# The weight-quarter sums of the FFN's seven products, from DVE to POOL

## The chip, the core and the metric

The kernel runs as one program on one core of a Trainium2 chip. The metric is the time of one execution on the device, in microseconds; the median of three runs is taken. The engines named below are those of the profile: PE multiplies matrices, PEld is its weight load, DVE is the vector engine, ACT the scalar engine, POOL the GpSimd engine, and SP issues the DMAs.

## What is computed

Two layers, each with a token mixer (retention, chunked attention and differential attention, gated and merged) and a feed-forward network (FFN). The change lies in the second product of the FFN, 512 tokens by 2816 hidden channels by 1024 model channels, in float32:

```python
for l in range(DEPTH):                         # 2 layers
    ...
    x = _layer_norm(DEEPNORM_ALPHA * x + mix, ln1_g[l], ln1_b[l])
    u = jnp.einsum('bsd,df->bsf', x, w_ffn_in[l])          # 512 x 1024 by 1024 x 5632
    u_gate, u_up = jnp.split(u, 2, axis=-1)
    ffn = jnp.einsum('bsf,fd->bsd', jax.nn.silu(u_gate) * u_up, w_ffn_out[l])
    x = _layer_norm(DEEPNORM_ALPHA * x + ffn, ln2_g[l], ln2_b[l])
```

## The kernel before

**Numbers as pairs.** A float32 operand is carried as a rounded part (`hi`, made on ACT) and what is left of it (`lo`, made on DVE). A product of two such operands is three matmuls, `mm3` in L106 to L108: hi by hi, and the two mixed products. A 512-column matmul is the unit of PE's work.

**Items.** The whole program is a list of items: the weight blocks that an item needs, and a function that does its matmuls. `run_items` keeps three blocks staged (`AHEAD`): at the start of an item it fetches the block of the item two further on. To fetch is to load float32 weights by DMA into one of three buffers `st`, cast them to `wh` on ACT and subtract to `wl` on DVE, each in two halves of 128x1024 elements. There are three buffers each of `wh` and `wl` too, so a cast waits until PE has done the item that last used its buffer. The compiler schedules the instructions of an engine; their order is not quite that of the source.

**The FFN.** The 2816 hidden channels are 22 blocks of 128. An item `u_ffn(i)` makes one of them from 48 matmuls, and `ffn_done` (L965 to L967) applies the gate. The last six blocks go through an ordinary product. The first sixteen form two groups of eight (`GROUPS`), and each group's share of the second product is made with seven products in place of eight (Winograd's form of Strassen's method): token halves and hidden halves on one side, quarters of the weight on the other.

**The hidden side.** When the second block of a pair is there, `Quarters` makes the sums of token halves (L217 to L220), and splits each into hi and lo. The part `q` is the plain quarter that product `m1` takes; its lo half is made by a DVE instruction at L98.

**The weight side.** `Halves` makes, for each group, the seven operands from four loaded quarters W(i, j) of 512x512 (i the half of the hidden rows, j the half of the output columns), each 128 partitions by 2048 elements. `b11` loads W(0,0) into a buffer of its own, `sa`, of which there is one. `t1` adds W(0,1) to it in place, and `t2` adds W(1,1) to that, in place again. `b21` and `b22` are plain quarters. `t3` is W(0,1) + W(1,1), made in the buffer of W(0,1), and `t4` is made from W(1,0) and the sum still in `sa`. Each sum is two instructions of 128x1024 elements on DVE (L163 and L195). `block` then casts and subtracts (`Staged`, L207 and L208).

**The order around the change.** Seven items `([operand], product)` from `fout_items`, in the order b11 with m1, t1 with y, t2 with x, b21, b22, t3, t4, each of 24 matmuls, alternate with `u_ffn` items of the next group (after the second group, with those of the last six blocks). In each layer both groups begin with m1, right behind the `u_ffn` item whose result is its last operand. The product with `t4` is "h"; `plus` adds products to the residual stream `z` or subtracts them.

Of the kernel before, what the change touches and what calls it, by code (L numbers as in the profile page):

```python
# [15 lines left out]
ALU = mybir.AluOpType  # L16
# [37 lines left out]
def trunk(ctx, tc, x_in, w_in, ret_norm_g, da_norm_g, lq1, lk1, lq2, lk2, w_a, w_b, w_c, b_merge, w_out,  # L54
          ln1_g, ln1_b, w_ffn_in, w_ffn_out, ln2_g, ln2_b, rel, rope_ret, rope_da, decay, out):
    nc = tc.nc
# [15 lines left out]
    def g(dt=F32, name="g"):  # L72
        return gp.tile([P, 512], dt, tag="g", name=name)
# [4 lines left out]
    def bank(name="ps"):  # L78
        return psp.tile([P, 512], F32, tag="ps", name=name)
# [25 lines left out]
    def mm3(ps, lh, ll, rh, rl, start, stop):  # L105
        nc.tensor.matmul(ps, lh, rh, start=start, stop=False)  # L106
        nc.tensor.matmul(ps, lh, rl, start=False, stop=False)  # L107
        nc.tensor.matmul(ps, ll, rh, start=False, stop=stop)  # L108
# [31 lines left out]
    class Halves:  # L140
# [19 lines left out]

        def add(self, t, u):
            for s in self.parts():
                nc.vector.tensor_add(t[:, s], t[:, s], u[:, s])  # L163

        def block(self, t):
            return Staged(t, self.kh, self.parts())
# [23 lines left out]
            return self.block(c)  # L190

        def t4(self):
            b, a = self.load(1, 0), self.__dict__.pop("a")
            for s in self.parts():
                nc.vector.scalar_tensor_tensor(b[:, s], a[:, s], -1.0, b[:, s], op0=ALU.mult, op1=ALU.subtract)  # L195
            return self.block(b)

    class Staged:
# [278 lines left out]
    def layer(l):  # L477
# [7 lines left out]
        v = {}  # L485
# [424 lines left out]
        def load_res(src):  # L910
            x1["z"] = [[g(name="z") for _ in range(2)] for _ in range(NT)]
            for t in range(NT):
                load_rows(x1["z"][t], src[P * t:P * t + P])
# [85 lines left out]
        def plus(t, hf, ps, op, final=False):  # L999

            z = x1["z"][t][hf]
            if (t, hf) in x2["fresh"]:
                x2["fresh"].remove((t, hf))
                nc.vector.scalar_tensor_tensor(z, z, ALPHA, ps, op0=ALU.mult, op1=op)
            else:
                nc.vector.tensor_tensor(z, z, ps, op=op)  # L1006
            if final:
                x2["n"].stats(t, hf)

        def fout_items(gi):  # L1010

            r0, kh = GROUPS[gi]
            hv = Halves(w_ffn_out[l], r0, kh)
            w = {}

            def run(name, j, wt):
                ps = bank("pf")
                for k in range(kh):
                    hi, lo = hid[r0 + k].use[name]
                    sl = slice(P * j, P * j + P)  # L1020
                    mm3(ps, hi[:, sl], lo[:, sl], wt.hi[:, k], wt.lo[:, k], k == 0, k == kh - 1)
                return ps

            def m1(wt):
                if gi == 0:
                    load_res(saved[2 * l])
                    x2["fresh"] = {(t, hf) for t in range(NT) for hf in range(2)}
                for j in range(2):
                    ps = run("m1", j, wt)
                    w[j] = g(name="w")  # L1030
                    nc.scalar.copy(w[j], ps)
                    plus(j, 0, ps, ALU.add)

            def y(wt):
                for j in range(2):
                    ps = run("y", j, wt)
                    w["y", j] = g(name="wy")
                    nc.scalar.copy(w["y", j], ps)

            def x(wt):  # L1040
                for j in range(2):
                    ps = run("x", j, wt)
                    u = w.pop(j)
                    nc.vector.tensor_sub(u, ps, u)
                    plus(2 + j, 0, u, ALU.subtract)
                    nc.vector.tensor_add(u, u, w.pop(("y", j)))
                    plus(2 + j, 1, u, ALU.add)
                    plus(j, 1, u, ALU.add)

            def one(name, i, hf, op):  # L1050
                def fn(wt):
                    for j in range(2):
                        plus(2 * i + j, hf, run(name, j, wt), op)
                return fn

            def gg(wt):
                for j in range(2):
                    ps = run("g", j, wt)
                    plus(2 + j, 1, ps, ALU.add)
                    plus(2 + j, 0, ps, ALU.subtract)  # L1060

            return [([hv.b11], m1), ([hv.t1], y), ([hv.t2], x), ([hv.b21], one("m2", 0, 0, ALU.add)),
                    ([hv.b22], one("v", 0, 1, ALU.add)), ([hv.t3], gg), ([hv.t4], one("h", 1, 0, ALU.subtract))]

        def fout_rest(hf):

# [41 lines left out]
        for gi, (r0, kh) in enumerate(GROUPS):  # L1108
            later = ids[:2 * GROUPS[gi + 1][1] if gi + 1 < len(GROUPS) else FT - REST]
            del ids[:len(later)]  # L1110
            for it in fout_items(gi):
                item(*it)
                if later:
                    item(*u_ffn(later.pop(0)))
            for i in later:
                item(*u_ffn(i))
# [60 lines left out]
```

## Time and profile before

| | us |
|---|---|
| median of three runs | 1956.7 (1955.91 to 1957.65) |
| the profiled execution, whole | 1958.14 |
| its span, first to last instruction | 1956.4 |
| PE busy in the span | 1932.8 |
| DVE busy | 1195.5 |
| ACT busy | 836.1 |
| POOL busy | 50.1 |
| mean granted PE clock | 0.997 |

The span is what the profile sees of the execution; the time of the execution holds 1.7 us more around it. PE's matmuls overlap one another, so a busy PE need not be one without small waits; those are read from the starts of its matmuls and from the waits of its weight loads.

### The profile page before, as it was taken

How to read it: one execution, taken by the hardware profiler on the slowest of the kernel's cores; microseconds unless marked ns; L12 is line 12 of the kernel's file. 1: busy time of each engine (PE TensorE's matmuls, PEld its weight loads, DVE VectorE, ACT ScalarE, POOL GpSimd, SP SyncE). 2: the span in 40 equal slices, each digit the busy share in tenths (PEclk: the TensorE clock that was granted, in tenths of full speed). 3: DMA queues.
4: the chain of work that ended last, by engine and by line, in shares of the span. 5: the costliest groups of instructions: out<-in, count | busy, mean ns of one | idle time of the engine just before them, and what ended most of it. 6: DMA issues, size and time to landing. Idle time of an engine off the chain costs nothing. (4 is left out here: it accounts for less than half of the span.)

```text
span 1956.4 us, 24330 instructions
## 1 busy us (share of the span) xinstructions
PE 1932.8 (99%) x9506; PEld 1634.9 (84%) x9506; DVE 1195.5 (61%) x2158; ACT 836.1 (43%) x1503; POOL 50.1 (3%) x73
## 2 busy tenths in 40 slices
PE   7999999999999999999999999999999999999998
PEld 7888888888888888888898888888888888888886
DVE  4654555577656666756585544655775575675656
ACT  3443445476533433333163344545664343432330
POOL 0000000000001000000000000000000000000000
PEclk9999999999999999999999999999999999999999
DMA  6322323222145444434442223222321543444341
GB/s 220 110 81 82 119 81 98 81 77 96 55 129 168 123 126 132 130 107 140 151 144 99 82 87 102 76 92 75 94 89 46 194 129 108 129 139 142 96 134 51
DMA packets 228535, 215.80 MB, mean 110 GB/s; under 512 B 7118, under 2 KB 179268, under 8 KB 228420
## 3 DMA queue, kind: packets, MB, share of 16 engines
q1 hardware_dynamic: 228420, 214.26, 34.9%
q8 instruction: 74, 1.21, 0.3%
q14 instruction: 41, 0.34, 0.1%
HBM read 205.84 MB, written 8.39 MB: 110 GB/s over the span
## 5 line engine op out<-in xcount | busy, mean ns | idle before, releaser
L106 PE MATMUL pt<-xTh,wh 128*128 128x512 f32 (+1 forms) x1632 | 604.2, 371 | 2.9 <-ACT xTh L90 2.9
L108 PE MATMUL pt<-xTh,wl 128*128 128x512 f32 (+1 forms) x1632 | 601.8, 369 | 0.0
L107 PE MATMUL pt<-xTl,wh 128*128 128x512 f32 (+1 forms) x1632 | 601.6, 369 | 0.2 <-DVE xTl L96 0.2
L136 DVE TENSOR_TENSOR wl<-st,wh 128x1024 fp32r<-128x1024 f32 (+1 forms) x314 | 354.3, 1145 | 177.8 <-ACT wh L135 177.6
L135 ACT CAST wh<-st 128x1024 fp32r<-128x1024 f32 (+1 forms) x314 | 301.8, 990 | 318.0 <-PE pt L107 156.7
L106 PEld LDWEIGHTS pt<-xTh,wh 128*128 128x128 f32 x1632 | 308.1, 189 | 53.1 <-ACT xTh L90 3.1
L108 PEld LDWEIGHTS pt<-xTh,wl 128*128 128x128 f32 x1632 | 308.4, 189 | 52.1 <-DVE wl L136 0.2
L107 PEld LDWEIGHTS pt<-xTl,wh 128*128 128x128 f32 x1632 | 308.7, 189 | 50.3 <-DVE xTl L96 0.5
L106 PE MATMUL pn<-wh,xTh 128*128 128x512 f32 x384 | 150.9, 393 | 0.0
L108 PE MATMUL pn<-wh,xTl 128*128 128x512 f32 x384 | 149.6, 390 | 0.0
L107 PE MATMUL pn<-wl,xTh 128*128 128x512 f32 x384 | 149.6, 390 | 0.0
L967 DVE TENSOR_TENSOR fth<-fth,pt 128x512 f32<-128x512 f32 x44 | 30.2, 687 | 128.6 <-PE pt L108 128.6
L108 PEld LDWEIGHTS pn<-wh,xTl 128*128 128x128 f32 x384 | 72.1, 188 | 15.2
L106 PEld LDWEIGHTS pn<-wh,xTh 128*128 128x128 f32 x384 | 72.1, 188 | 14.1
L107 PEld LDWEIGHTS pn<-wl,xTh 128*128 128x128 f32 x384 | 72.2, 188 | 14.1
L965 ACT ACTIVATE fth<-pt 128x512 f32<-128x512 f32 x44 | 26.3, 598 | 122.8 <-PE pt L108 122.8
L269 ACT COPY sw<-pt 32x512 f32<-32x512 f32 (+1 forms) x96 | 55.6, 580 | 31.0 <-PE pt L108 29.7
L966 DVE SCALAR_TENSOR_TENSOR fth<-fth,pt 128x512 f32<-128x512 f32 x44 | 30.2, 686 | 62.6 <-ACT fth L965 62.6
L207 ACT CAST wh<-st 128x1024 fp32r<-128x1024 f32 x32 | 32.1, 1050 | 74.4 <-PE pt L107 74.4
L321 ACT ACTIVATE cE<-cE,mx 128x512 f32<-128x512 f32 (+1 forms) x64 | 35.3, 553 | 65.1 <-DVE mx L320 65.1
L106 PE MATMUL pt<-oah,wh 128*128 128x512 f32 x128 | 50.8, 397 | 0.0
L108 PE MATMUL pt<-oah,wl 128*128 128x512 f32 x128 | 50.0, 390 | 0.0
(234 smaller groups left out, 3019.4 us busy)
## 6 DMA issues: line engine op xcount, KB each, us to landing
st<-in_w_in SPq DMA_DIRECT2D x55, 1024.0 KB
st<-in_w_ffn_in SPq DMA_DIRECT2D x88, 512.0 KB
st<-in_w_ffn_out SPq DMA_DIRECT2D x28, 1024.0 KB
st<-in_w_in SPq DMA_DIRECT2D x32, 512.0 KB
st<-in_w_branch_a SPq DMA_DIRECT2D x8, 1024.0 KB
st<-in_w_out SPq DMA_DIRECT2D x8, 1024.0 KB
saved<-z SPq DMA_DIRECT2D x24, 256.0 KB
z<-saved SPq DMA_DIRECT2D x24, 256.0 KB
```

The lines of the kernel that those rows point to most:

```text
L106: nc.tensor.matmul(ps, lh, rh, start=start, stop=False)
L107: nc.tensor.matmul(ps, lh, rl, start=False, stop=False)
L108: nc.tensor.matmul(ps, ll, rh, start=False, stop=stop)
L135: nc.scalar.copy(self.hi[:, a:b], st[:, a:b])
L136: nc.vector.tensor_sub(self.lo[:, a:b], st[:, a:b], f(self.hi[:, a:b]))
L207: nc.scalar.copy(self.hi[:, s], st[:, s])
L269: nc.scalar.copy(sw[half * b:half * b + half], ps[half * o:half * o + half])
L321: nc.scalar.activation(e, e, AF.Exp, bias=nm, accum_out=sums[:, nt:nt + 1])
L965: nc.scalar.activation(t, pg, AF.Tanh, scale=0.5)
L966: nc.vector.scalar_tensor_tensor(t, t, 1.0, pg, op0=ALU.add, op1=ALU.mult)
L967: nc.vector.tensor_mul(t, t, pu)
```

## The change

The four sums of each group move to POOL, and `t4` becomes the plain sum W(1,0) plus the sum in `sa`, where it was that sum negated. Product h is then added where it was subtracted. So 24 instructions at L163 change their engine, and 8 at L195 change engine and operation; the number of instructions and their sizes stay.

```diff
         def add(self, t, u):
             for s in self.parts():
-                nc.vector.tensor_add(t[:, s], t[:, s], u[:, s])
+                nc.gpsimd.tensor_add(t[:, s], t[:, s], u[:, s])
...
         def t4(self):
-            b, a = self.load(1, 0), self.__dict__.pop("a")
-            for s in self.parts():
-                nc.vector.scalar_tensor_tensor(b[:, s], a[:, s], -1.0, b[:, s], op0=ALU.mult, op1=ALU.subtract)
+            b = self.load(1, 0)
+            self.add(b, self.__dict__.pop("a"))
             return self.block(b)
...
             return [([hv.b11], m1), ([hv.t1], y), ([hv.t2], x), ([hv.b21], one("m2", 0, 0, ALU.add)),
-                    ([hv.b22], one("v", 0, 1, ALU.add)), ([hv.t3], gg), ([hv.t4], one("h", 1, 0, ALU.subtract))]
+                    ([hv.b22], one("v", 0, 1, ALU.add)), ([hv.t3], gg), ([hv.t4], one("h", 1, 0, ALU.add))]
```

## The prediction, written before the result was known

> **What bounds the kernel now.** I read the page's busy times first, then the busy time by stage, then the tile `q` with what waited for it, then PE's and DVE's timelines where that wait is.
>
> ```profile
> PE 1932.8 (99%) x9506; PEld 1634.9 (84%) x9506; DVE 1195.5 (61%) x2158; ACT 836.1 (43%) x1503; POOL 50.1 (3%) x73
> ...
> 740.00:890.00 150.00, 150.00 (x662) 123.99 (x662) 97.74 (x129) 53.24 (x69) 0.00 (x0) 1.00 0.41 120
> 1700.00:1890.00 190.00, 190.00 (x840) 157.09 (x839) 121.40 (x154) 66.34 (x84) 0.00 (x0) 1.00 0.42 127
> ```
>
> PE is the bound. In the two stretches where the sums lie (span, then PE, weight load, DVE, ACT, POOL busy), PE is busy all of the time: 662 matmuls in 150 us, one every 0.227 us. DVE is at 65% and POOL does nothing. So the 32 sums that leave DVE free no time by themselves. PE can only lose, or win back waits too small to make it idle, and the profile shows one kind of these:
>
> ```profile
> its engine sat idle before it (us, times) until:
>   DVE q L98: 1.2, 4
> who waited for it (us, times):
>   PEld pf L108: 1.2, 4
> ...
> 724.00 0.39 PE L107 MATMUL pf<-wl,q 128*128 128x512 f32 x1
> 724.26 0.73 PE L108 MATMUL pf<-wh,q 128*128 128x512 f32 x2
> 724.83 0.40 PE L106 MATMUL pt<-xTh,wh 128*128 128x512 f32 x1
> ...
> 1816.42 0.73 PE L108 MATMUL pf<-wh,q 128*128 128x512 f32 x2
> ```
>
> Four times, once per group and layer, the last two matmuls of product m1 wait 0.3 us each time for the lo half of `q` from DVE. At 724.26 they follow their forerunner by 0.26 us instead of 0.227. This is a place without slack: every microsecond that DVE is later with `q` is a microsecond of PE. What DVE does just ahead of it:
>
> ```profile
> 721.18 1.22 DVE L208 TENSOR_TENSOR wl<-sa,wh 128x1024 fp32r<-128x1024 f32 x1
> 722.32 0.42 DVE L219 TENSOR_TENSOR sb<-fth,sa 128x256 f32<-128x256 f32 x1
> 722.65 1.22 DVE L208 TENSOR_TENSOR wl<-sa,wh 128x1024 fp32r<-128x1024 f32 x1
> 723.79 0.42 DVE L98 SCALAR_TENSOR_TENSOR q<-fth,q 128x256 fp32r<-128x256 f32 x1
> 724.73 1.22 DVE L163 TENSOR_TENSOR sa<-sa,st 128x1024 f32<-128x1024 f32 x1
> ...
> 1815.95 0.42 DVE L98 SCALAR_TENSOR_TENSOR q<-fth,q 128x256 fp32r<-128x256 f32 x1
> ```
>
> DVE ends `q` at 723.79 + 0.42 = 724.21, and the matmul starts 0.05 us later. The two L208 make `wl` from t1 in `sa`, and the sum for t2 overwrites `sa`, half by half. On DVE that sum came behind `q`, at 724.73. It needs only the first L208, which ends at 721.18 + 1.22 = 722.40.
>
> **The change part by part.** What it removes:
>
> ```profile
> L163 DVE TENSOR_TENSOR sa<-sa,st x16: 1215/1219/1228, 703.0 to 1822.7; 128x1024 f32<-128x1024 f32 x16
> L163 DVE TENSOR_TENSOR st<-st x8: 1218/1220/1227, 772.4 to 1865.9; 128x1024 f32<-128x1024 f32 x8
> L195 DVE SCALAR_TENSOR_TENSOR st<-sa,st x8: 1218/1222/1227, 783.2 to 1877.0; 128x1024 f32<-128x1024 f32 x8
> ```
>
> DVE loses 16 x 1.219 + 8 x 1.220 + 8 x 1.222 = 39.0 us. None of it lies ahead of a wait of PE (the sum at 724.73 is behind `q`), so it is worth nothing; 1.2 us, the four waits together, is the most that could be won. The sign of t4 and of h changes no instruction's size: nothing.
>
> What it adds is 32 sums on POOL. No such sum is in this trace. The nearest rows:
>
> ```profile
> 0.73 0.20 POOL masks.py:197 MEMSET ident<- 128x128 f32 x1 [0.29 <-POOLq L1166]
> 0.87 0.10 POOL L69 MEMSET mhalf<- 128x4 f32 x1
> 1.15 0.29 POOL masks.py:199 TENSOR_SCALAR_AFFINE_SELECT ident<-ident 128x128 f32<-128x128 f32 x1
> ```
>
> Writing costs (0.20 - 0.10) / 124 = 0.8 ns a column; reading one operand and writing costs (0.29 - 0.10) / 124 = 1.5 ns, so a read adds about 0.7 ns. Two reads and a write are 2.2 to 2.3 ns, or 2.3 to 2.4 us for 1024 columns with 0.1 us of start. From below, the write alone would be 0.8 us; from above, twice the one-operand price is 3.2 us. I take 2.3 us, from the row with a read in it. The Trainium skill, "GPSIMD Engine Reference", section 3.1, measures a 2048-column fp32 add at 4.497 us against 2.293 on the vector engine; half of that, an estimate from the page, is 2.25 us, and no row here shows it.
>
> *Is the staging still in time?* Now an item's cast on ACT waits for POOL, and the cast's neighbours on ACT queue behind it. The rows of the tightest sums:
>
> ```profile
> 735.77 2.00 ACT L207 CAST wh<-sa 128x1024 fp32r<-128x1024 f32 x2 [4.60 <-PE pt L107]
> ...
> 772.37 2.36 DVE L163 TENSOR_TENSOR st<-st 128x1024 f32<-128x1024 f32 x2
> ...
> 783.15 2.36 DVE L195 SCALAR_TENSOR_TENSOR st<-sa,st 128x1024 f32<-128x1024 f32 x2 [2.37 <-DMA st<-in_w_ffn_out]
> ...
> 784.73 2.00 ACT L207 CAST wh<-st 128x1024 fp32r<-128x1024 f32 x2 [4.66 <-PE pt L107]
> ...
> 801.05 2.01 ACT L207 CAST wh<-st 128x1024 fp32r<-128x1024 f32 x2 [4.66 <-PE pt L107]
> ```
>
> t2 may start at 722.4 and is cast at 735.77: 13.3 us for 4.6. t3 has from 772.37 at the latest to 784.73, 12.3 us. t4 waits for its data until 783.15 and has 17.9 us. Behind each cast stand another 10 us and more: PE takes the block two items after its buffer came free, 48 + 24 matmuls or 16.3 us later, and the cast (2.0) and the subtraction (two of 1.22) take about 4.5. So the sums themselves are hidden by PE, even at twice the price. The loads that wait for a buffer which a sum reads move by 2 or 3 us inside the same slack. On POOL's own queue nothing waits behind a sum but other sums:
>
> ```profile
> 970.60 0.54 POOL L379 TENSOR_TENSOR rs<-rs,mhalf 128x1 f32<-128x1 f32 x1 [334.93 <-DVE rs L378]
> ```
>
> *What does a sum on POOL do to the DVE instructions beside it?* Here is the price of the change. The trace has small POOL instructions that read, beside DVE:
>
> ```profile
> 610.67 0.55 POOL L379 TENSOR_TENSOR rs<-rs,mhalf 128x1 f32<-128x1 f32 x1 [69.45 <-DVE rs L378]
> ...
> 624.74 0.69 DVE L422 TENSOR_TENSOR z<-z,bc 128x512 f32<-128x512 f32 x1
> 625.33 2.36 DVE L136 TENSOR_TENSOR wl<-st,wh 128x1024 fp32r<-128x1024 f32 x2
> 627.61 0.43 DVE L96 TENSOR_TENSOR xTl<-lnt,xTh 128x256 fp32r<-128x256 f32 x1
> 624.90 3.53 POOL L379 TENSOR_TENSOR rs<-rs,mhalf 128x1 f32<-128x1 f32 x1 [6.42 <-DVE rs L378]
> ...
> 982.15 0.68 DVE L422 TENSOR_TENSOR z<-z,bc 128x512 f32<-128x512 f32 x1
> 982.75 2.36 DVE L136 TENSOR_TENSOR wl<-st,wh 128x1024 fp32r<-128x1024 f32 x2
> 982.37 0.85 POOL L379 TENSOR_TENSOR rs<-rs,mhalf 128x1 f32<-128x1 f32 x1 [5.32 <-DVE rs L378]
> ```
>
> Alone, the one-column power takes 0.55 us (610.67). Beside a DVE instruction that reads two SBUF tensors it ends 0.39 us after that instruction: 982.37 + 0.85 = 983.22, against L422's end at 982.83. At 624.90 it got through only when the whole run of such instructions was over: it ends at 628.43, the last of them at 628.04. So POOL's read and DVE's two-tensor read exclude each other for the length of an instruction; POOL may get in between two of them (982.83) or be passed over at three boundaries (625.43 to 627.7). What a long POOL read does to DVE, this trace cannot show: POOL read one column here. From below it costs DVE nothing; from above, DVE stands until the sum is done, up to 3.2 us. I take the second kind at the likely price, since what excludes in one direction by whole instructions should do so in the other.
>
> Now the four places. The first half of t2's sum is released at 722.40 and asks for its operands while L219 (two SBUF tensors) runs, until 722.74. If POOL gets in there, the second L208 begins at 722.74 + 2.3 = 725.04 instead of 722.65, 2.4 us late, and `q` with it. If POOL is passed over there and gets in at the next boundary, between L208 and `q`, `q` is late by as much. The second half of the sum waits for the second L208 and comes too late to get ahead of `q`. So m1's last two matmuls start 2.3 us late (between 2.4 and a little less, as a part of POOL's 2.3 us is start-up): 4 x 2.3 = **9.2 us**. Nothing gives this back, as PE has no idle time behind it. Elsewhere a DVE delay of 2.3 us lies inside the 10 us above.
>
> The Trainium skill, "SBUF — State Buffer", section "Who interferes with whom", says that a vector instruction with two SBUF inputs contends with a GpSimd instruction that reads SBUF, and that whichever starts first holds the shared port for its whole instruction. The first direction agrees with the power that ended 0.39 us after DVE; the case at 624.90, passed over three times, doesn't fit a strict order of issue. By the rule the sum here is the 9.2 us above; without it, nothing.
>
> **The sum.** 0 for the work removed, 0 for the staging, + 9.2 for four delays of `q`. The profiled execution (1958.14, span 1956.4 and 1.7 around it) would become 1967.3; it lies 1.4 above the median of the runs, so the runs should have a median of 1956.7 + 9.2 = **1965.9 us**.
>
> **The rivals.**
>
> *DVE keeps the port until `q` is through, or POOL gives way within its sum.* Then the change is invisible: 1956.7, 1955.5 at best. For it: at 624.90 DVE kept POOL out over three boundaries, and only two lie ahead of `q`. Against: at 982.83 POOL got in at the first, between the same kinds of instruction.
>
> *The two share the port.* If DVE goes at half speed beside POOL, the second L208 and `q` (1.64 us together) lengthen by 0.8 to 1.6 us less the overlap; some 0.8 us at four places is 3 us, 1960. No row speaks for it: a one-column read would not have to wait for an instruction's end.
>
> *It gets faster.* For 4 us or more PE would have to be waiting somewhere for DVE, and only 1.2 us of such waits is there. A changed order of instructions would have to bring it.
>
> *Staging late.* If POOL's sums are starved by DVE's dense runs, a cast comes late. It decides from the point where two halves of t2 take over 13 us (cast) plus 10 (PE): 11 us for one half where I count 2.3. Each further microsecond would be one of PE, in up to 16 items; at 1 us each, 1972.7. DVE at 65%, with pauses such as the 2.37 us before 783.15, makes it unlikely.
>
> *The change doesn't do what it says.* All 32 sums go through the edited lines, so DVE must fall by 39 us; I see no way around that.
>
> **How the numbers follow.** Delay of `q` by whole sums: 0.55. DVE first or POOL yielding: 0.30. Shared: 0.09. Staging late: 0.03. Faster: 0.03. A measurement of this kernel tells about 0.2%, or 3.9 us, from no change. Slower by more: 0.55 + 0.03 + 0.02 of the shared case = 0.60. Within: 0.30 + 0.07 = 0.37. Faster: 0.03. The delay case alone reaches from four delays of 1.5 us (POOL holding DVE up only for its two reads, 2 x 0.7 ns x 1024) to four of 3.1 (the dear sum without its start), 1962.7 to 1969.1. To take in the second case, without which over 2 in 10 would be left out, the range goes from 1955.8 to 1969.5.
>
> **What would show it.** Right: POOL has 32 more instructions; one of them begins at each of the four places about 0.1 us after the first L208; the second L208 or `q` ends some 2.3 us late; and PEld's wait for `q` is 9 to 10 us over four times, not 1.2. DVE instructions beside POOL look longer than 1.22 us, or begin late. Wrong: PEld's wait for `q` stays at 1.2 us; or POOL's halves last much longer than 2.4 us at these places and begin or end only behind `q`. If the compiler places `q` ahead of the second L208, the argument falls too.

## The result and the profile after

| | before | after |
|---|---|---|
| median of four runs, us | 1956.45 (1955.91 to 1957.65) | 1970.46 (1967.56 to 1971.22) |
| span of the profiled execution, us | 1956.4 | 1969.4 |

The ratio is 1.0068, with a 95% interval from 1.0051 to 1.0085: the changed kernel is 14.0 us slower. Line numbers behind L195 are one lower in it; L208 is now L207. In the experiments the numbers shift with each edit, so the same subtraction is L207 to L210 there.

The page's busy times, and the POOL sums in the groups by line (busy time, mean duration in ns, idle time before them):

```profile
PE 1939.0 (98%) x9506; PEld 1638.7 (83%) x9506; DVE 1210.5 (61%) x2126; ACT 835.9 (42%) x1503; POOL 133.1 (7%) x105
...
L163 POOL TENSOR_TENSOR sa<-sa,st 128x1024 f32<-128x1024 f32 x16 | 41.1, 2574 | 270.3 <-DVE wl L207 270.3
L163 POOL TENSOR_TENSOR st<-st,sa 128x1024 f32<-128x1024 f32 x8 | 22.2, 2795 | 42.3 <-DMA st<-in_w_ffn_out 42.3
L163 POOL TENSOR_TENSOR st<-st 128x1024 f32<-128x1024 f32 x8 | 22.1, 2781 | 180.2 <-DMA st<-in_w_ffn_out 180.2
```

All 32 sums are on POOL, at 2.6 to 2.8 us each. DVE has 32 instructions fewer, and yet it is busy 15 us longer (1210.5 for 1195.5): those that are left have become longer. What waited for `q`, in the view of that tile:

```profile
its engine sat idle before it (us, times) until:
  DVE q L98: 18.2, 8
who waited for it (us, times):
  ACT wh L135: 15.7, 4
  PEld pf L108: 9.9, 4
  PE pf L108: 8.3, 4
```

The weight load now waits 9.9 us for `q`, four times, where it waited 1.2. PE's own 8.3 us are the same four waits, seen at the matmul. The timelines of DVE and POOL at the first place (start, duration, instruction):

```profile
719.98 1.22 DVE L207 TENSOR_TENSOR wl<-sa,wh 128x1024 fp32r<-128x1024 f32 x1
721.11 0.42 DVE L218 TENSOR_TENSOR sb<-fth,sa 128x256 f32<-128x256 f32 x1
721.45 3.41 DVE L207 TENSOR_TENSOR wl<-sa,wh 128x1024 fp32r<-128x1024 f32 x1
724.78 0.41 DVE L98 SCALAR_TENSOR_TENSOR q<-fth,q 128x256 fp32r<-128x256 f32 x1
725.12 2.87 DVE L98 SCALAR_TENSOR_TENSOR q2l<-fth,q2h 128x512 fp32r<-128x512 f32 x1
```
```profile
721.27 2.50 POOL L163 TENSOR_TENSOR sa<-sa,st 128x1024 f32<-128x1024 f32 x1 [15.57 <-DVE wl L207]
724.94 2.50 POOL L163 TENSOR_TENSOR sa<-sa,st 128x1024 f32<-128x1024 f32 x1 [1.16 <-DVE wl L207]
```

The first half of t2's sum begins 0.07 us after the end of the first L207 (719.98 + 1.22 = 721.20), while L218 runs. Then the second L207 takes 3.41 us in place of 1.22: it is held for 2.19 us, and `q` comes that much later. POOL's sum ends at 721.27 + 2.50 = 723.77, and the subtraction 1.09 us after that: DVE stood until POOL was through. The second half of the sum begins while `q` runs and holds the next instruction, q2l, for which PE does not wait. Then PE:

```profile
722.80 0.39 PE L107 MATMUL pf<-wl,q 128*128 128x512 f32 x1
725.25 0.73 PE L108 MATMUL pf<-wh,q 128*128 128x512 f32 x2 [2.06 <-DVE q L98]
...
726.20 0.63 PE L107 MATMUL pt<-xTl,wh 128*128 128x512 f32 x1
726.63 0.63 PE L108 MATMUL pt<-xTh,wl 128*128 128x512 f32 x1
727.05 0.63 PE L106 MATMUL pt<-xTh,wh 128*128 128x512 f32 x1
...
729.70 0.39 PE L107 MATMUL pt<-xTl,wh 128*128 128x512 f32 x1
```

Up to the wait, and again from 729.5 on, a matmul begins every 0.227 us. Between 726.20 and 727.05 it is 0.43 us. Less than a microsecond behind its wait PE fell to half speed, and it kept that for some microseconds. The busy times by stretch have the granted clock with it; the columns are span, PE, weight load, DVE, ACT and POOL, each with its instructions, then the granted clock:

```profile
722.46:725.87 3.41, 1.35 (x7) 0.80 (x6) 3.41 (x3) 0.00 (x0) 2.25 (x2) 1.00 0.00 0
725.87:729.28 3.41, 3.41 (x10) 2.67 (x9) 3.41 (x4) 2.96 (x4) 1.57 (x1) 0.50 0.06 10
729.28:732.70 3.42, 3.42 (x17) 2.82 (x16) 2.18 (x2) 0.00 (x0) 0.00 (x0) 1.00 1.05 391
```

For the 3.41 us from 725.87 on, the granted clock is 0.50. In them 10 matmuls run instead of 17 (each count takes in those that overlap an edge), so 7 x 0.227 = 1.6 us are lost. The clock is halved for one such stretch behind each of the four waits of this execution.

**Where the time went.** The waits are 9.9 - 1.2 = 8.7 us. The four halved stretches are 4 x 1.6 = 6.4 us. Together that is 15.1 us, for a span that is 13.0 us longer. Of the difference, 1.5 us is in the other waits of the weight load (18.2 us in sum before, 16.7 after), which lie outside the FFN's sums. The last 0.6 us by which the parts are too large stays unassigned; the profile before has a halved stretch of its own near its start (shown further down), where the changed one has the full clock, and what that is worth was not measured.

### The profile page after: what moved, and what is told of

It is laid out like the page before. It is cut to its first block, busy times and chain, and to the rows that moved or that the text cites. A ratio compares the mean times of both kernels' runs of the same rounds, so it can differ in the third digit from the quotient of the medians.

```text
span 1969.4 us, 24355 instructions
## 1 busy us (share of the span) xinstructions
PE 1939.0 (98%) x9506; PEld 1638.7 (83%) x9506; DVE 1210.5 (61%) x2126; ACT 835.9 (42%) x1503; POOL 133.1 (7%) x105
## 5 line engine op out<-in xcount | busy, mean ns | idle before, releaser
L966 DVE TENSOR_TENSOR fth<-fth,pt 128x512 f32<-128x512 f32 x44 | 30.2, 687 | 143.5 <-PE pt L108 143.3
L163 POOL TENSOR_TENSOR sa<-sa,st 128x1024 f32<-128x1024 f32 x16 | 41.1, 2574 | 270.3 <-DVE wl L207 270.3
L207 DVE TENSOR_TENSOR wl<-st,wh 128x1024 fp32r<-128x1024 f32 x32 | 51.0, 1625 | 2.6 <-ACT wh L206 2.6
```

What stands on the lines that cost most here:

```text
L163: nc.gpsimd.tensor_add(t[:, s], t[:, s], u[:, s])
L207: nc.vector.tensor_sub(self.lo[:, s], st[:, s], f(self.hi[:, s]))
L966: nc.vector.tensor_mul(t, t, pu)
```

## The experiments

The theory after the traces: the whole loss is the first half of t2's sum getting ahead of `q`, in the four places, and PE pays for the wait twice, by its length and by a halved clock behind it. The first rival is that every sum on POOL costs its share; the second, that t2 gives the four waits alone and the other sums the rest.

**Only t2 back on DVE** (t1, t3 and t4 stay on POOL):

```diff
         def t2(self):
-            self.add(self.a, self.load(1, 1))
+            u = self.load(1, 1)
+            for s in self.parts():
+                nc.vector.tensor_add(self.a[:, s], self.a[:, s], u[:, s])
```

> Changed kernel with the sum for t2 back on DVE; t1, t3 and t4 stay on POOL (24 of the 32 sums). Theory (the whole loss is the first half of t2's sum holding DVE up ahead of q, and what PE loses by that wait): 1956.5, within 2 us of before, and the weight load waits for q about 1.2 us over four times. Rival 1 (every sum on POOL costs its share, by holding DVE up or by late staging): three quarters of the 14 us stay, about 1967. Rival 2 (only the four waits come from t2, some 9 us, and the rest from the other sums): about 1961.

Measured: 1957.05 us, ratio to before 0.9998 (0.9989 to 1.0008). The tile `q`:

```profile
  PEld pf L108: 1.2, 4
```

The wait is that of before, and 24 sums on POOL cost nothing that can be measured. Both rivals fall. The sums do hold DVE up here too (the longest subtraction from `sa` still takes 3.42 us), but PE waits for nothing that comes late by it. So it is the place of the hold that costs.

**Only t2 on POOL**, the same edit the other way round in the kernel before: `nc.gpsimd.tensor_add` for t2, the other sums on DVE.

> Kernel before with only the sum for t2 on POOL (8 of the 32 sums). Theory: the whole loss, 1968 to 1971, with four waits of 2.5 us for q and the clock halved for 3.4 us behind each. Rival 1 (every sum its share): a quarter of it, 1960. Rival 2: 1965.5, without the part that the other sums bring.

Measured: 1968.08 us, ratio 1.0055 (1.004 to 1.007). The wait for `q` and the DVE timeline at the first place:

```profile
  PEld pf L108: 9.9, 4
```
```profile
721.87 3.41 DVE L210 TENSOR_TENSOR wl<-sa,wh 128x1024 fp32r<-128x1024 f32 x1
```

Eight of the 32 sums bring the whole of the waits, to a tenth of a microsecond, and 11.3 of the 14.0 us. One thing was not as expected: in this profile the clock is halved behind one of the four waits only, and the span is 1965.7. That led to the last run below, the changed kernel once more.

**t2 as one sum of 2048 columns**, all sums on POOL. It must wait for both subtractions from `sa`:

```diff
         def t2(self):
-            self.add(self.a, self.load(1, 1))
+            u = self.load(1, 1)
+            nc.gpsimd.tensor_add(self.a, self.a, u)
```

> Changed kernel, all sums on POOL, but t2's as one instruction of 2048 columns, which must wait for both subtractions from sa and so starts when q is already running on DVE. Theory: no wait of PE, 1956.5 within 2 us, though POOL adds as much as in the changed kernel. Rivals 1 and 2 (work on POOL costs by its amount): 1965 to 1971. If POOL got ahead of q after all, the wait would be about 5 us and the time near 1980.

Measured: 1956.84 us, ratio 0.9998 (0.9988 to 1.0008). DVE and POOL at the first place:

```profile
723.04 1.22 DVE L208 TENSOR_TENSOR wl<-sa,wh 128x1024 fp32r<-128x1024 f32 x1
724.17 0.42 DVE L98 SCALAR_TENSOR_TENSOR q<-fth,q 128x256 fp32r<-128x256 f32 x1
```
```profile
724.34 6.53 POOL L178 TENSOR_TENSOR sa<-sa,st 128x2048 f32<-128x2048 f32 x1 [17.04 <-DVE wl L208]
```

The sum now starts while `q` runs, `q` keeps its 0.42 us, and the loss is gone. POOL does the same work. What costs is when it starts, not how much it is. This is the change as it could have been made, and it is as fast as the kernel before, not faster: DVE's freed time had no taker.

**A shorter first part.** Two kernels cut t2's sum so that less of it can get ahead of `q`: 512 columns and then 1536, or 768 and then the rest in two pieces. The 512 cut:

```diff
         def t2(self):
-            self.add(self.a, self.load(1, 1))
+            u = self.load(1, 1)
+            for s in (slice(0, 1), slice(1, self.kh)):
+                nc.gpsimd.tensor_add(self.a[:, s], self.a[:, s], u[:, s])
```

> Changed kernel with t2's sum cut into 512 and 1536 columns: the part that can get ahead of q is half as long. Theory for the wait: q is 1.25 to 1.3 us late at four places, 5 us. Clock part, first reading (the clock is halved for 3.4 us behind a wait only if the wait fills most of such a stretch): not at 1.3 us, so 1961.5. Second reading (any wait of a microsecond brings it): 1.7 us more at each place, 1968. If the loss does not go with the length of the first part: 1970.

> Changed kernel with 768 columns of t2's sum first (the rest waits for both subtractions). Between 512 columns (waits of 1.4 us, no halved clock) and 1024 (2.5 us, halved behind some or all): the waits should be 1.9 to 2.0 us, 6.5 us more than before in sum. Clock theory with a chance that grows with the wait: none to two of the four places with the clock halved, at 1.6 us each: 1963 to 1966.5. If the clock is only a matter of 2 us and more: 1963.3.

Measured: 1961.32 us (ratio 1.0023, 1.0013 to 1.0032) and 1963.84 us (1.0031, 1.0017 to 1.0044). The second subtraction on DVE, the first part on POOL and the wait, with 512 columns first:

```profile
720.87 2.31 DVE L209 TENSOR_TENSOR wl<-sa,wh 128x1024 fp32r<-128x1024 f32 x1
```
```profile
720.69 1.41 POOL L179 TENSOR_TENSOR sa<-sa,st 128x512 f32<-128x512 f32 x1 [15.57 <-DVE wl L209]
```
```profile
  PEld pf L108: 5.5, 4
```

and with 768:

```profile
721.14 2.88 DVE L209 TENSOR_TENSOR wl<-sa,wh 128x1024 fp32r<-128x1024 f32 x1
```
```profile
720.96 1.97 POOL L179 TENSOR_TENSOR sa<-sa,st 128x768 f32<-128x768 f32 x1 [15.57 <-DVE wl L209]
```
```profile
  PEld pf L108: 7.8, 4
```

The waits go with the length of the first part. In neither profile is the clock halved behind a wait, and the times are near those expected for that: 1961.5 with 512 columns, by the first reading, and 1963.3 with 768.

**Which part of POOL's work holds DVE?** In two kernels made from the kernel before, the sum for t2 is left out: `sa` is set to zero by POOL, or overwritten with the loaded quarter, in the same two halves released at the same moment. The edits are shown against the kernel with t2 alone on POOL; with the memset the quarter is not loaded either.

```diff
-                nc.gpsimd.tensor_add(self.a[:, s], self.a[:, s], u[:, s])
+                nc.gpsimd.memset(self.a[:, s], 0.0)
...
-                nc.gpsimd.tensor_add(self.a[:, s], self.a[:, s], u[:, s])
+                nc.gpsimd.tensor_copy(self.a[:, s], u[:, s])
```

> Kernel before, with t2's sum left out and both halves of sa set to zero by POOL, released by the same subtraction at the same moment. If POOL's reads are what holds DVE up: DVE's subtraction keeps its 1.22 us, no wait beyond the old 1.2 us in total, 1956.8. If any POOL instruction with 1024 columns holds it up: about 0.8 to 1 us late at four places, 1960 to 1961.

> Kernel before, with t2's sum replaced by a copy of the loaded quarter into sa on POOL: one operand read where the sum reads two. Reads theory, each read taking its time on the port: the copy lasts 1.0 to 1.7 us, DVE's subtraction is as much longer, and with four waits of that length the time is 1961 to 1963.5. If a copy's single read goes past DVE's: 1956.8. If the hold has a fixed length: 1966 or more.

Measured: 1957.1 us with the memset (ratio 1.0, 0.9991 to 1.001), 1960.52 with the copy (1.0017, 1.0008 to 1.0027). DVE and POOL with the memset:

```profile
721.54 1.21 DVE L209 TENSOR_TENSOR wl<-sa,wh 128x1024 fp32r<-128x1024 f32 x1
```
```profile
721.34 0.96 POOL L178 MEMSET sa<- 128x1024 f32 x1 [86.78 <-DVE wl L209]
```

With the copy, DVE's subtraction, POOL's copies as a group, and the wait:

```profile
721.42 2.06 DVE L210 TENSOR_TENSOR wl<-sa,wh 128x1024 fp32r<-128x1024 f32 x1
```
```profile
L179 POOL COPY sa<-st 128x1024 f32<-128x1024 f32 x8 | 9.3, 1161 | 423.6 <-DVE wl L210 423.6
```
```profile
  PEld pf L108: 4.5, 4
```

A write of 0.96 us beside DVE costs DVE nothing; one read stream holds it for 2.06 - 1.22 = 0.84 us, two streams for 2.19. In all four kernels whose POOL instruction reads, the hold is that instruction's length less 0.31 or 0.32 us: 0.84 of 1.16 for the copy, 1.09 of 1.41, 1.66 of 1.97 and 2.19 of 2.50 for the sums. The copy's length lay in the 1.0 to 1.7 us expected. DVE's subtraction was to be longer by all of it and was longer by 0.84 us, so the time lay half a microsecond under the expectation.

**Not every DVE instruction is held.** The changed kernel's own trace shows the other side, where t4's sum runs beside a gate product, which reads one operand from PSUM (`pt`):

```profile
1889.77 0.69 DVE L966 TENSOR_TENSOR fth<-fth,pt 128x512 f32<-128x512 f32 x1 [4.12 <-PE pt L108]
1890.67 2.54 DVE L207 TENSOR_TENSOR wl<-st,wh 128x1024 fp32r<-128x1024 f32 x1 [0.21 <-ACT wh L206]
1893.13 3.41 DVE L207 TENSOR_TENSOR wl<-st,wh 128x1024 fp32r<-128x1024 f32 x1
```
```profile
1889.71 2.41 POOL L163 TENSOR_TENSOR st<-st,sa 128x1024 f32<-128x1024 f32 x1 [10.46 <-DMA st<-in_w_ffn_out]
1892.08 3.38 POOL L163 TENSOR_TENSOR st<-st,sa 128x1024 f32<-128x1024 f32 x1
```

L966 keeps its 0.69 us inside POOL's first sum, and that sum its 2.41. Then the two take turns, and each holds the other: the first subtraction, with both operands in SBUF, ends 1.09 us after POOL's first sum (1893.21 and 1892.12); POOL's second sum, begun while that subtraction runs, takes 0.97 us longer than its first; and the second subtraction ends 1.08 us after the second sum. The two subtractions take 5.87 us instead of 2.36.

**When is the clock halved?** The changed kernel, once more:

> The changed kernel once more, for the clock alone. The four waits should be 2.5 us each again. If the halved clock behind a wait depends on where the wait falls in the clock's own stretches of 3.4 us, this execution has another number of halved places than four, and its time goes with it by 1.6 us each; if it belongs to the wait, four again and 1970 to 1971.

Measured: 1968.45 us, span 1966.6, waits of 9.9 us again, and the clock halved behind the second and the fourth wait. That is two halved stretches fewer than in the first profile, 3.2 us by the count, for an execution 2.8 us shorter (1971.22 there). In both profiles of the changed kernel the halved stretches lie whole multiples of 3.413 us apart, on a grid; for a kernel with fewer of them behind the waits, the grid is taken from whatever halved stretches its trace has. A wait is PE's idle time between the last matmul ahead of `q` and the next: 2.06 us in these two profiles and in that of t2 alone. Here are the stretch that holds the larger part of a wait, and the next, for two waits of this run, one of the kernel with t2 alone, and one of that with 768 columns:

```profile
850.03:853.44 3.41, 1.35 (x6) 0.96 (x6) 3.41 (x3) 0.32 (x1) 2.25 (x2) 1.00 0.00 0
853.44:856.85 3.41, 3.41 (x10) 2.66 (x9) 3.41 (x4) 2.64 (x4) 1.06 (x1) 0.50 0.21 62
1822.83:1826.24 3.41, 1.54 (x7) 1.28 (x8) 3.41 (x3) 0.73 (x1) 2.25 (x2) 1.00 0.01 2
1826.24:1829.65 3.41, 3.41 (x10) 2.64 (x9) 3.41 (x4) 2.23 (x4) 0.65 (x1) 0.50 0.43 113
```
```profile
851.34:854.75 3.41, 1.60 (x7) 1.34 (x8) 3.41 (x3) 0.80 (x1) 2.25 (x2) 1.00 0.00 0
854.75:858.16 3.41, 3.41 (x17) 2.81 (x16) 3.41 (x4) 2.17 (x4) 0.60 (x1) 1.00 0.43 107
```
```profile
1693.07:1696.48 3.41, 1.88 (x9) 1.44 (x9) 3.41 (x4) 0.94 (x1) 2.25 (x3) 1.00 0.01 2
1696.48:1699.89 3.41, 3.41 (x17) 2.81 (x16) 3.41 (x3) 2.03 (x4) 1.58 (x1) 1.00 0.12 13
```

Read the second column of each first line. After a stretch in which PE was busy for 1.35 or 1.54 us, the next has the clock at 0.50; after one with 1.60 or 1.88 it stays at 1.00. A wait of 2.06 us halves the clock if nearly all of it falls into one stretch (1.87 us of idle time or more), and does not if an edge of the grid cuts off a quarter of a microsecond (1.81 us or less is left). The clock was halved at 4, 2 and 1 of the four places in the three profiles. A wait of 1.53 us alone cannot empty a stretch that far, wherever it falls. The limit is less sharp than these places make it: elsewhere, a stretch with PE busy for 1.54 us (768 columns, from 1594.08) and one with 1.47 (t2 back on DVE, from 1945.41) were followed by the full clock.

The grid does not start with the program: a halved stretch begins at 725.87 in the first profile of the changed kernel and at 853.44 in the second, 37.4 stretches apart. That would explain why the changed kernel's runs spread over 3.7 us, and their mean granted clocks go with it: 0.997 in the run of 1967.56 us, 0.996 in that of 1969.85, 0.995 in those of 1971.08 and 1971.22, where one halved stretch makes up 3.41 x 0.5 / 1969 = 0.0009 of it.

All the kernels in one table. The waits are the weight load's, less the 1.2 us of before; the time is against the median of before in the same set of runs (1956.83, or 1957.37 for the copy and 768 columns; 1956.45 for the changed kernel):

| what gets ahead of `q` | DVE held, us | waits over before, us | clock halved | time over before, us |
|---|---|---|---|---|
| copy, 1024 columns | 0.84 | 3.3 | 0 of 4 | 3.2 |
| sum, 512 | 1.09 | 4.3 | 0 of 4 | 4.5 |
| sum, 768 | 1.66 | 6.6 | 0 of 4 | 6.5 |
| sum, 1024, t2 alone | 2.19 | 8.7 | 1 of 4 | 11.3 |
| sum, 1024, all on POOL | 2.19 | 8.7 | 4 of 4, 2 of 4 | 14.0 |

Up to 768 columns the time is the sum of the waits, to within 0.2 us, closer than the intervals of some 2 us either way could promise. At 1024 it is 2.6 and 5.3 us more. Halved stretches of 1.6 us each can make that up, a varying number of them (1.6 and 3.3 on average); how many the executions without a kept trace had is not shown.

## Where the prediction was right, and the step that failed

*PE is the bound, and DVE's 39 us are worth nothing.* Right: with t2 elsewhere, or started later, the sums on POOL leave the time as it was.

*The staging is hidden.* Right. Sums took 2.4 to 3.4 us, PE waited for none of their casts, and 24 of them cost nothing. The rival of late staging did not come about.

*A sum on POOL holds DVE up for its length.* Right, and now in the direction that the trace before couldn't show. The price was taken as 2.3 us; the hold was 2.19 and the sum 2.50. That they agree so well is in part luck: the reads were priced at 0.7 us each, and they cost 0.2 and 1.3 (last section). POOL got in at the first boundary in all four places.

*Four places, 2.3 us each, 9.2 us.* Right in place and mechanism: the waits grew by 8.7 us. The rivals in which DVE keeps the port, or shares it, are out: at half speed the subtraction could not have become longer by more than its own 1.22 us, and it became longer by 2.19.

*"Nothing gives this back", and so the sum is 9.2.* Here it failed: "every microsecond that DVE is later with `q` is a microsecond of PE" prices a wait at its length and no more. The term that it lacks is what PE loses behind the wait: nothing, or 1.6 us at each place, by how the wait falls on the clock's grid; 6.4 us in the profiled execution, and 5.3 us between the waits and the median of the four runs. So the range's upper end, built from the longest hold alone, was too low by a microsecond, and the forecast by 4.6 us. The trace before had the clue, near its start, in the busy times by stretch:

```profile
24.40:27.81 3.41, 0.91 (x8) 0.94 (x9) 0.00 (x0) 0.00 (x0) 0.00 (x0) 1.00 1.05 391
27.81:31.22 3.41, 3.41 (x18) 3.41 (x18) 0.51 (x2) 0.86 (x3) 0.00 (x0) 0.50 1.05 389
```

PE waits there for the first inputs, is busy for 0.91 us of a stretch, and has half the clock in the next. I read the clock as a constant and never asked what a new idle time would do to it.

The Trainium skill, "TensorE: Matmul & The Clock Gate", section "What's actually happening", describes a clock that falls to half after an idle window of a free-running 3413 ns monitor. The grid of 3.413 us and the factor agree with these traces. Its advice, in "Why this matters for your kernels", to keep PE's idle gaps under some 3 us does not: gaps of 2.06 us were enough here, where a stretch was left less than half busy.

## What to carry to other kernels

Find the places where the bounding engine waits with no slack, even for 0.3 us, and ask of each change what may now start just ahead of them: work moved off an engine starts earlier than it did there, and can hold up what it was moved away from. Look at what the work that starts reads, too, and not at its length alone; here the same sum released one instruction later was free. Price a new wait of PE at its length plus the clock: here waits of up to 1.53 us cost their length alone, and those of 2.06 us up to 1.6 us more each.

## What was not expected of the hardware

A wait of PE of 2.06 us halved its clock afterwards in 7 of 12 places. At these places the limit lay between 1.54 and 1.60 us of PE's busy time in a stretch of 3.41; two stretches elsewhere, with 1.47 and 1.54, kept the full clock.

POOL's hold on DVE goes with what POOL reads: 0.84 us for one stream of 1024 columns, 2.19 for two, none for a write of the same size. A one-read copy of 1.16 us on POOL is barely slower than the write alone (0.96), so the sum of single prices by which the prediction estimated a sum (0.7 ns a column for each read) was too even: the second read costs 1.3 us, the first 0.2.
